# A new order inside the even attention steps of a two-layer encoder kernel

## The chip, the cores and the metric

The kernel runs on one core of a Trainium2 chip. The metric is device time in microseconds (us) of one execution of the whole program. Each kernel is run several times, and the median is given.

## What is computed

An encoder trunk of two layers over 1024 tokens of width 1024. Layer 0 mixes tokens by neighbourhood attention (mixer A), layer 1 by grouped-query attention (mixer B). Each layer is followed by an output projection and a gated per-layer embedding. The part that matters here is mixer B, for one block of 128 queries:

```python
def q_block(qb):          # 16 query heads in 4 groups, head dimension 64, 1024 keys
    sc = jnp.einsum('bkgqd,bksd->bkgqs', qb, k).astype(jnp.float32) * scale
    pr = jax.nn.softmax(sc, axis=-1).astype(v.dtype)
    return jnp.einsum('bkgqs,bksd->bkgqd', pr, v)
...
return (o * jax.nn.silu(gate)) @ w_out
```

q and k are RMS-normalised for each head and rotated by the token's row and column before this. All products are made at nearly full fp32 precision: each operand is split in a high and a low part (`h` and `l` in the tiles' names), and the products of the parts are summed.

## The kernel before

The program has four stages in a row: `mixer_a`, `dense_phase(0)`, `mixer_b`, `dense_phase(1)`. There is no automatic scheduler: every engine executes its instructions in the order in which the Python code issues them, and waits for the other engines by semaphores. So the order in which functions are called is the order of each engine's queue.

**Steps of mixer B.** The attention work is cut in 128 steps (`steps`, L1059). Step n is one head h, one half hf of the tokens and one tile t of 128 queries in this half; four steps in a row make one head's half, eight make a pair of heads' half. The functions of a step are

- `f_S` (L1061), the scores: four TensorE (PE) matmuls of 512 columns in a PSUM tile `s` (two buffers), and the row minimum `mn` on VectorE (DVE, L1071; q is negated, so that the minimum is the maximum);
- `f_E` (L1074), the exponential: ScalarE (ACT, L1077) reads `s` and `mn` and writes P, with the row's sum accumulated;
- `f_T` (L1080), P's transposes: eight PE transposes in two PSUM tiles `t` (L1087; the pool has two buffers), each tile copied by ACT to PTh (L1089) and the rest taken by DVE to PTl (L1090). PTh and PTl have room for two steps, an even and an odd one;
- `f_AV` (L1095), the product with v: sixteen PE matmuls for two steps at once, in the PSUM tile `o` (one buffer). It is issued in an even step n, for steps n-2 and n-1. Where it ends a head's half, `head_end` (L434) is called.
- `q_stack` (L1036), once in eight steps: four PE transposes of q (L1041) in a tile of the same pool `t`, an ACT copy (L1043), and, some issues later, the high part (ACT, L1050) and the low part (DVE, L1051) of the two tiles QS that the scores of the next eight steps read.

In step n the kernel issues T(n), E(n+1) and S(n+2). In even steps the order is AV, E, T, S; in odd steps T, E, S and, where (n + QS_AT) is a multiple of 8, `q_stack`.

**The end of a head.** `head_end` posts `evac`: ACT copies the lower half of `o` (L482), DVE adds the upper half (`join`, L446), which sets `o` free, and DVE takes the reciprocal of the row sums (L472). For the last pair of heads the reciprocal is spread (L459) and transposed by PE (`across`, L465) in another tile `o`.

**Dense work in between.** `mix` (L338) runs the list `att` of the steps' functions, each with a weight, and puts chunks of the dense work (projections of q, k, v, gate and of the embedding, in PSUM tile `d`, one buffer) between them: after each function it issues dense chunks until their share of the total is that of the weights so far. CB holds the weights of an even step's functions, CN those of an odd one. Each dense chunk is 6 or 12 matmuls; the last of a tile also issues the tile's copies on ACT.

**Pulses and the weight slot.** After each function `pulse` runs: `WQ.pump` may turn one staged weight tile (512 KB, loaded by a DMA in SP's queue) into its high part `wh` (ACT, L220), and issues the low part `wl` (DVE, L221) at the next pulse; `post.tick` counts down postponed work. `WQ.gate` says whether a weight may be split: None always, True yes, False only where a dense chunk needs it at once. In the loop it is True from an odd step's scores up to the next step's first function, so that a split falls right behind S(odd). From step 112 on it is None.

The lines that set the gate and the order, in short:

```python
te = [(f_T(n), w[2]), (f_E(n+1), w[3])]
if n % 2 == 0:
    te.reverse()
...
f_S(*steps[n + 2])
WQ.gate = n % 2 == 1 if n < 112 else None
```

Of the kernel before, what the change touches and what calls it, by code (L numbers as in the profile page):

```python
# [27 lines left out]
BIG = 1e30  # L28
WSLOTS = 4
CA = (1.0, 0.5, 1.25, 1.0, 0.75)  # L30
CB = (1.25, 1.0, 2.0, 0.5, 1.0)
CN = (1.5, 0.0, 1.0, 1.0, 1.5)
DG, DR, DQ, DY, NP = 1, 2, 2, 1, 8
KT, KN = 2, 4
DO = (2, 3)
DD = ((3, 2), (3, 2))
DT = (5, 2)
FIN = (4, 4)
# [1 line left out]
DP = 1  # L40
KD, KS = 3, 4
QD = (2, 5, 8)
QS_AT = 5
QO = (4, 6)
AGE, LAG = 3, 3
YS = (11, 11)
# [108 lines left out]
def trunk(ctx, tc, x, wts, rpb, gains, hgains, mask, rope, out):  # L155
# [21 lines left out]
    class Weights:  # L177
# [29 lines left out]
        def pump(self, force=False):  # L207
            self.clock += 1
            self.settle()
            self.stage(force)  # L210
            if self.split >= self.staged:
                return
            key, pid = self.q[self.split]
            if not force and self.gate is False:
                return
            if self.live[pid] >= self.cap[pid] or not (force or self.clock - self.st[key][1] >= self.age):
                return
            s, _ = self.st.pop(key)
            hi, lo = self.alloc[pid]()
            act.activation(hi, s, AF.Copy)  # L220
            self.rest = lambda: dve.tensor_tensor(lo, s, hi, ALU.subtract)  # L221
            self.tiles[key] = (hi, lo, pid)
            self.live[pid] += 1
            self.split += 1
            self.last = self.clock

        def settle(self):
            if self.rest:
# [17 lines left out]
    WQ = Weights()  # L246
# [187 lines left out]
    def head_end(sb, h, hf, rs, Ops, ylive, layer, gg, talloc):  # L434
        pair = h // 2
        b = (h % 2) * 64
        if h % 2 == 0:
            Y = sb.tile([128, 512], F32, name="Y", bufs=2)
            rb = sb.tile([128, 512], F32, name="rb", bufs=2)
            r8 = sb.tile([128, 8], F32, name="r8", bufs=4)  # L440
            ylive[pair, hf] = (Y, rb, r8, {})
        Y, rb, r8, tail = ylive[pair, hf]
        yh = Y[b:b + 64]

        def join():
            dve.scalar_tensor_tensor(yh, Ops[0:64], 0.5, yh, op0=ALU.mult, op1=ALU.add)  # L446

        def rows():
            r8T = sb.tile([128, 32], F32, name="r8T", bufs=2)
            dve.transpose(r8T.rearrange("p (a c) -> p a c", a=4), r8[:, None].to_broadcast([128, 4, 8]))  # L450
            rD = dram.tile([8, 128], F32, name="rD", bufs=4)
            for b in range(4):
                post.add(DD[layer][1], lambda b=b: sync.dma_start(rD[:, 32 * b:32 * b + 32], r8T[32 * b:32 * b + 8]))
            for i in range(2):
                post.add(DD[layer][1], lambda i=i: sync.dma_start(
                    rb[64 * i:64 * i + 64], bass.AP(tensor=rD.tensor, offset=rD.offset + 512 * i, ap=[[0, 64], [1, 512]])))

        def spread():
            dve.tensor_copy(rb.rearrange("p (t j c) -> p t j c", t=4, j=2),  # L459
                            r8.rearrange("p (j t) -> p t j", j=2)[:, :, :, None].to_broadcast([128, 4, 2, 64]))  # L460

        def across():
            ps = talloc()
            for t in range(4):
                pe.transpose(ps[:, t], rb[:, t * 128:(t + 1) * 128], ident)  # L465
            ps = ps.rearrange("p t c -> p (t c)")
            if hf == 0:
                act.activation(rb, ps, AF.Copy)
            tail["rb"] = rb if hf == 0 else ps

        def norm():
            dve.reciprocal(r8[:, 4 * (h % 2):4 * (h % 2) + 4], rs)  # L472
            if h % 2 == 0:
                return
            if pair < 7:
                post.add(DD[layer][0], rows)
            else:
                spread()
                post.add(DT[hf], across)

        def evac():
            act.activation(yh, Ops[64:128], AF.Copy, scale=0.5)  # L482
            post.add(DY, join)
            norm()
        if h == NH - 1 and hf == 1:
            evac()
        else:
            post.add(DO[layer], evac)
        if h % 2 == 0:
            return None  # L490
        G = gg.pop((pair, hf))
        del ylive[pair, hf]

        def fin_last():
            dve.tensor_tensor(Y, Y, G, ALU.mult)
            if "rb" not in tail:
                post.l = [e for e in post.l if e[1] is not across]
                across()
            dve.tensor_tensor(Y, Y, tail["rb"], ALU.mult)
            y3 = Y.rearrange("p (t c) -> p t c", t=4)  # L500
            ts = slice(4 * hf, 4 * hf + 4)
            act.activation(HTh[:, ts, 7, :], y3, AF.Copy)
            dve.tensor_tensor(HTl[:, ts, 7, :], y3, HTh[:, ts, 7, :], ALU.subtract)

        def fin():
            yhi, ylo = rb.bitcast(F32R), Y.bitcast(F32R)

            def store(c, src):
                sync.dma_start(yD[layer][c][4 * hf:4 * hf + 4, :, pair, :].rearrange("t p c -> p t c"),
                               src.rearrange("p (t c) -> p t c", t=4))  # L510

            def split():
                act.activation(yhi, Y, AF.Copy)
                dve.tensor_tensor(ylo, Y, yhi, ALU.subtract)
                post.add(2, lambda: (store(0, rb), store(1, Y)))
            pool.tensor_tensor(Y, Y, G, ALU.mult)
            pool.tensor_tensor(Y, Y, rb, ALU.mult)
            post.add(YS[layer], split)
        return fin_last if pair == 7 else fin
# [340 lines left out]
    def mixer_b(pend):  # L860
        with ExitStack() as es:
# [249 lines left out]
            pre = kv[:-2] + qi[:6] + kv[-2:-1] + qi[6:10] + kv[-1:] + qi[10:14]  # L1111
            fill = qi[14:] + [d for hf in range(2) for d in gate_items("bg", 0, hf, dalloc, sb, gg)]
            pre += [glue(lambda: q_stack(0, 0))] + fill[:5]
            pre += [glue(lambda: f_S(*steps[0]))] + fill[5:6] + [glue(lambda: f_E(*steps[0]))] + fill[6:7]
            pre += [glue(lambda: f_S(*steps[1]))] + fill[7:]
            for i, d in enumerate(pre):
                if i >= 2 and i % 2 == 0 and pend:
# [6 lines left out]
            for g in range(4):  # L1124
                att = []
                for n in range(32 * g, 32 * g + 32):
                    h, hf, t = steps[n]
                    av = n >= 2 and n % 2 == 0
                    w = CB if av else CN
                    def turn():  # L1130
                        if WQ.gate:
                            WQ.gate = False
                        later.tick()
                    att.append((turn, w[0]))
                    if av:
                        att.append((lambda n=n: f_AV(*steps[n - 1]), w[1]))
                    te = [(lambda n=n: f_T(*steps[n]), w[2])]
                    if n + 1 < len(steps):
                        te.append((lambda n=n: f_E(*steps[n + 1]), w[3]))
                    if n % 2 == 0:  # L1140
                        te.reverse()
                    att += te
                    if n + 2 < len(steps):
                        def scores(n=n):
                            f_S(*steps[n + 2])
                            WQ.gate = n % 2 == 1 if n < 112 else None
                        att.append((scores, w[4]))
                    m = n + QS_AT
                    if m % 8 == 0 and m < len(steps):
                        hn, fn, _ = steps[m]  # L1150
                        att.append((lambda hn=hn, fn=fn: q_stack(hn // 2, fn), 0.0))
                    if YLOAD_B <= n < YLOAD_B + NT:
                        att.append((lambda t=n - YLOAD_B: load_y(1, t), 0.0))
                if g == 3:
                    att.append((lambda: f_AV(*steps[-1]), CB[1]))
                def gates(p):
                    return [i for hf in range(2) for i in gate_items("bg", p, hf, dalloc, sb, gg)]
                dense = []
                if g > 0:
                    dense += left  # L1160
                if g < 3:
                    qi = q_items(g + 1, pool)
                    kv = kv_items(1, pool) if g == 1 else [None, None]
                    dense += kv[:-2] + qi[:KS] + [k for k in kv[-2:-1] if k] + qi[KS:8] + [k for k in kv[-1:] if k] + gates(2 * g + 1) + qi[8:]
                    left = gates(2 * g + 2)
                else:
                    WQ.cap[3] = 2
                    dense += gates(2 * g + 1) + pp_items(1, dalloc, sb, TAGS_B)
                mix(att, dense, hold=HOLD if g == 3 else 0)
# [170 lines left out]
```

## Time and profile before

| | before |
|---|---|
| median of 3 runs | 1563.97 us (1562.44 to 1564.62) |
| the profiled execution | 1560.76 us |
| its span, from the first to the last instruction | 1558.9 us |
| mean granted TensorE clock | 0.998 |
| loop of mixer B (first scores to the last product with v) | 784 to 1361 us of the span |
| TensorE busy from 1086 to 1221 us | 135.0 of 135.0 us |
| TensorE busy from 1221 to 1361 us | 134.83 of 140 us |

In the rows below, PE is TensorE, PEld its weight loads, DVE VectorE, ACT ScalarE, POOL GpSimd, SP SyncE. A row of the groups reads: line, engine, operation, what it writes and reads, shapes, count, then the busy time, the mean ns of one, and the engine's idle time before it with what ended it. A row of the waits reads: who waited for whom, us in total, times, longest. A row of the timeline begins with the start in us and the duration; in square brackets stand the engine's idle time before it and what ended it. Matmuls are pipelined, and their ends are modelled.

### The profile page before, as it was taken

What the parts mean: (1) busy time and instruction counts of PE and PEld (TensorE: products, weight loads), DVE (VectorE), ACT (ScalarE), POOL (GpSimd) and SP (SyncE); (2) the same over time, 40 slices, a digit from 0 to 9 for tenths busy, and PEclk for the clock granted to TensorE, in tenths of its full rate; (3) what the DMA queues carried; (4) which work ended last, traced back from release to release, by engine and by line L of the source; (5) the groups of instructions that cost most, each with busy time, mean ns of one, the idle gap of its engine ahead of it and who ended that gap; (6) DMA issues with size and microseconds to landing.
All of it is one profiled execution on the core that took longest, in us unless ns stands there. A gap on an engine that the chain in (4) does not pass through costs nothing.

```text
span 1558.9 us, 24287 instructions
## 1 busy us (share of the span) xinstructions
PE 1519.0 (97%) x9048; PEld 1327.7 (85%) x9048; DVE 1025.8 (66%) x2062; ACT 871.8 (56%) x1744; POOL 279.5 (18%) x372
## 2 busy tenths in 40 slices
PE   6999999999999999999999999999999999999997
PEld 5888988988988788888988889989999888788886
DVE  6576477377477436648877787777877877625636
ACT  6465466376366622434466776766767777622422
POOL 2111121112112010000222132443131200000023
PEclk9999999999999999999999999999999999999999
DMA  8212122132122972142210111111111113651213
GB/s 274 78 41 75 44 89 79 35 95 82 35 85 83 336 260 68 54 141 94 76 49 21 39 38 55 45 38 50 56 33 42 61 55 117 225 200 54 75 55 128
DMA packets 89861, 138.84 MB, mean 89 GB/s; under 512 B 16912, under 2 KB 55952, under 8 KB 89744
## 3 DMA queue, kind: packets, MB, share of 16 engines
q1 hardware_dynamic: 85136, 122.62, 24.3%
q10 hardware_dynamic: 4608, 14.68, 2.6%
q8 instruction: 71, 1.16, 0.3%
q14 instruction: 46, 0.38, 0.1%
HBM read 104.65 MB, written 36.15 MB: 90 GB/s over the span
## 4 chain that ended last, share of the span: by engine, by line
PE 43%; DVE 6%; ACT 3%; issue 2%; ACTq 0%; DVEq 0%
PE d L305 23%; PE o L305 7%; PE t L1087 6%; PE s L305 6%; DVE PTl L1090 1%; DVE mn L1071 1%; ACT PTh L1089 1%; ACT P L1077 1%; PE t L430 1%; PE t L1041 0%; DVE QS L1051 0%; DVE wl L221 0%; DVE t L905 0%; DVE KB L982 0%; DVE qt L906 0%
## 5 line engine op out<-in xcount | busy, mean ns | idle before, releaser
L305 PE MATMUL d<-wh,HTh 128*128 128x256 f32 (+1 forms) x1096 | 372.6, 340 | 4.8 <-ACT HTh L431 2.1
L305 PE MATMUL d<-wh,HTl 128*128 128x256 f32 (+1 forms) x1096 | 365.9, 334 | 1.5 <-DVE HTl L432 1.5
L305 PE MATMUL d<-wl,HTh 128*128 128x256 f32 (+1 forms) x1096 | 365.2, 333 | 0.0
L1090 DVE TENSOR_TENSOR PTl<-t,PTh 128x512 fp32r<-128x512 f32 x256 | 164.5, 684 | 107.1 <-ACT PTh L1089 106.7
L305 PEld LDWEIGHTS d<-wh,HTh 128*128 128x128 f32 x1096 | 207.9, 190 | 28.2 <-ACT HTh L431 2.7
L305 PEld LDWEIGHTS d<-wh,HTl 128*128 128x128 f32 x1096 | 207.8, 190 | 24.0 <-DVE HTl L432 2.2
L305 PEld LDWEIGHTS d<-wl,HTh 128*128 128x128 f32 x1096 | 208.2, 190 | 21.4
L305 PE MATMUL d<-HTh,wh 128*128 128x512 f32 x504 | 206.0, 409 | 0.0
L305 PE MATMUL d<-HTh,wl 128*128 128x512 f32 x504 | 197.8, 392 | 0.0
L305 PE MATMUL d<-HTl,wh 128*128 128x512 f32 x504 | 197.7, 392 | 0.0
L1077 ACT ACTIVATE P<-s,mn 128x1024 f32<-128x1024 f32 x128 | 142.8, 1116 | 56.6 <-DVE mn L1071 55.7
L1089 ACT ACTIVATE PTh<-t 128x512 fp32r<-128x512 f32 x256 | 140.1, 593 | 45.8 <-PE t L1087 45.3
L1071 DVE TENSOR_REDUCE mn<-s 128x1 f32<-128x1024 f32 x128 | 154.9, 1210 | 11.9 <-PE s L305 11.8
L1087 PE MATMUL t<-ident,P 128*128 128x128 f32 x1024 | 136.9, 274 | 6.6 <-DVE PTl L1090 4.8
L221 DVE TENSOR_TENSOR wl<-wstage,wh 128x1024 fp32r<-128x1024 f32 x89 | 115.1, 1298 | 42.3 <-ACT wh L220 42.1
L305 PE MATMUL s<-KA,QS 128*128 128x512 f32 (+2 forms) x384 | 133.5, 402 | 0.0
L1087 PEld LDWEIGHTS t<-ident,P 128*128 128x128 f32 x1024 | 114.8, 140 | 21.7 <-DVE PTl L1090 15.8
L305 PE MATMUL s<-KB,QS 128*128 128x512 f32 (+2 forms) x384 | 121.8, 371 | 0.0
L305 PE MATMUL o<-PTh,V 128*128 128x256 f32 (+2 forms) x672 | 118.8, 287 | 1.5 <-DVE Y L446 0.9
L305 PE MATMUL o<-PTl,V 128*128 128x256 f32 (+2 forms) x672 | 119.3, 289 | 0.4 <-DVE PTl L684 0.3
L684 DVE TENSOR_TENSOR PTl<-t,PTh 128x384 fp32r<-128x384 f32 (+1 forms) x128 | 66.6, 521 | 76.1 <-ACT PTh L683 75.0
L305 PEld LDWEIGHTS d<-HTh,wl 128*128 128x128 f32 x504 | 94.6, 188 | 21.8
(179 smaller groups left out, 2483.6 us busy)
## 6 DMA issues: line engine op xcount, KB each, us to landing
wstage<-in_wts SPq DMA_DIRECT2D x92, 512.0 KB
X<-in_x SPq DMA_DIRECT2D x16, 512.0 KB
pp<-ppD SPq DMA_DIRECT2D x32, 256.0 KB
rb<-rD SPq DMA_DIRECT2D x56, 128.0 KB
ppD<-th SPq DMA_DIRECT2D x20, 256.0 KB
xD<-X SPq DMA_DIRECT2D x8, 512.0 KB
X<-xD SPq DMA_DIRECT2D x8, 512.0 KB
yD0h<-rb SPq DMA_DIRECT2D x14, 256.0 KB
```

Source lines behind the costliest of these rows:

```text
L221: self.rest = lambda: dve.tensor_tensor(lo, s, hi, ALU.subtract)
L305: pe.matmul(ps, a, b, start=first, stop=last, skip_group_check=True)
L430: pe.transpose(ps[:, k], xn[:, (4 * c + k) * 128:(4 * c + k + 1) * 128], ident)
L684: dve.tensor_tensor(PTl[:, sl], ps[:, :m], PTh[:, sl], ALU.subtract)
L1071: dve.tensor_reduce(mn, ps, axis=AX.X, op=ALU.min)
L1077: act.activation(p, ps, AF.Exp, bias=mn, scale=-1.0, accum_out=RS[h, hf][:, t:t + 1])
L1087: pe.transpose(ps[:, i], p[:, k * 128:(k + 1) * 128], ident)
L1089: act.activation(PTh[:, ks, c], ps, AF.Copy)
L1090: dve.tensor_tensor(PTl[:, ks, c], ps, PTh[:, ks, c], ALU.subtract)
```

## The change

In even steps the exponential E(n+1) comes first, then (where due) q's transposes, then AV, T, S: `q_stack` moves from the end of an odd step to an even one (QS_AT 4 in place of 5). Odd steps keep T, E, S. The gate opens with an even step's E and closes with its T, and also closes after one split; it is closed too from the first scores in the prologue on. In layer 1 a head's end is evacuated two pulses after its last product instead of three (the same place, since E has left the row of functions in between), and the join is issued at once with it, ahead of the next scores' minimum, instead of one pulse later. The weights are put down anew as CE and CO; their sums for a pair of steps stay as they were, but the very last step's first function has the weight LAST, and the last product with v 1.5 instead of 1.0.

```diff
-CB = (1.25, 1.0, 2.0, 0.5, 1.0)
-CN = (1.5, 0.0, 1.0, 1.0, 1.5)
+CE = (1.25, 0.0, 1.5, 2.0, 1.0)
+CO = (1.5, 1.0, 1.0, 1.5)
+LAST = 4.0
-DO = (2, 3)
+DO = (2, 2)
-QS_AT = 5
+QS_AT = 4
...
             self.last = self.clock
+            if self.gate:
+                self.gate = False
...
             act.activation(yh, Ops[64:128], AF.Copy, scale=0.5)
-            post.add(DY, join)
+            if layer == 0:
+                post.add(DY, join)
             norm()
+            if layer == 1:
+                join()
...
-            pre += [glue(lambda: f_S(*steps[0]))] + fill[5:6] + [glue(lambda: f_E(*steps[0]))] + fill[6:7]
+            def first():
+                f_S(*steps[0])
+                WQ.gate = False
+            pre += [glue(first)] + fill[5:6] + [glue(lambda: f_E(*steps[0]))] + fill[6:7]
...
-                    h, hf, t = steps[n]
-                    av = n >= 2 and n % 2 == 0
-                    w = CB if av else CN
-                    def turn():
-                        if WQ.gate:
-                            WQ.gate = False
-                        later.tick()
-                    att.append((turn, w[0]))
-                    if av:
-                        att.append((lambda n=n: f_AV(*steps[n - 1]), w[1]))
-                    te = [(lambda n=n: f_T(*steps[n]), w[2])]
-                    if n + 1 < len(steps):
-                        te.append((lambda n=n: f_E(*steps[n + 1]), w[3]))
+                    def exp(n=n):
+                        f_E(*steps[n + 1])
+                        WQ.gate = n % 2 == 0 if n < 112 else None
+
+                    def turn(n=n):
+                        f_T(*steps[n])
+                        if WQ.gate:
+                            WQ.gate = False
+                    ahead = [exp] if n + 1 < len(steps) else []
+                    scores = [lambda n=n: f_S(*steps[n + 2])] if n + 2 < len(steps) else []
                     if n % 2 == 0:
-                        te.reverse()
-                    att += te
-                    if n + 2 < len(steps):
-                        def scores(n=n):
-                            f_S(*steps[n + 2])
-                            WQ.gate = n % 2 == 1 if n < 112 else None
-                        att.append((scores, w[4]))
-                    m = n + QS_AT
-                    if m % 8 == 0 and m < len(steps):
-                        hn, fn, _ = steps[m]
-                        att.append((lambda hn=hn, fn=fn: q_stack(hn // 2, fn), 0.0))
+                        fs = list(zip([later.tick] + ahead, CE))
+                        m = n + QS_AT
+                        if m % 8 == 0 and m < len(steps):
+                            hn, fn, _ = steps[m]
+                            fs.append((lambda hn=hn, fn=fn: q_stack(hn // 2, fn), 0.0))
+                        if n >= 2:
+                            fs.append((lambda n=n: f_AV(*steps[n - 1]), CE[2]))
+                        fs += zip([turn] + scores, CE[3:])
+                    else:
+                        fs = list(zip([later.tick, turn] + ahead + scores, CO))
+                        if n == len(steps) - 1:
+                            fs[0] = (later.tick, LAST)
+                    att += fs
...
-                    att.append((lambda: f_AV(*steps[-1]), CB[1]))
+                    att.append((lambda: f_AV(*steps[-1]), CE[2]))
```

## The prediction, made before the changed kernel ran

> **What bounds the kernel now.** The page's first part comes first, then the waits of TensorE inside mixer B's loop (from 760 us to 1370 us), since the change touches nothing else.
>
> ```profile
> PE 1519.0 (97%) x9048; PEld 1327.7 (85%) x9048; DVE 1025.8 (66%) x2062; ACT 871.8 (56%) x1744; POOL 279.5 (18%) x372
> ```
> ```profile
> PE t L1087 <- DVE PTl L1090: 4.8, 4, 1.6
> PE t L1041 <- DVE PTl L1090: 1.9, 4, 0.9
> PE t L1087 <- ACT th L976: 1.2, 2, 0.8
> PE o L465 <- DVE Y L446: 1.0, 1, 1.0
> PE o L305 <- DVE Y L446: 0.9, 2, 0.6
> ```
>
> TensorE (PE) is the bound: 1519.0 of 1558.9 us. In the loop its named waits are 4.8 + 1.9 + 1.2 + 1.0 + 0.9 = 9.8 us. The order of its work hardly changes, so the most that a better order can bring is about 10 us; what it can cost is open above. So the question is which PE waits go and which come.
>
> What sits just behind PE? The rows over the steps' stretch (795 to 1358 us) show the exponential E and its accumulator read:
>
> ```profile
> L1077 ACT ACTIVATE P<-s,mn 128x1024 f32<-128x1024 f32 x127 | 141.7, 1115 | 52.3 <-DVE mn L1071 51.4
> ...
> L1077 ACT ACTIVATION_READ_ACCUMULATOR P<-s,mn 128x1 f32 x127 | 25.1, 197 | 0.0
> ```
>
> ScalarE (ACT) stands idle 51.4 us ahead of E, and what ends the idleness is the row minimum `mn` on VectorE (DVE), not ACT's queue. Step 64 (write n for a step's number) shows the chain:
>
> ```profile
> 1086.22 1.07 ACT L220 ACTIVATE wh<-wstage 128x1024 fp32r<-128x1024 f32 x1
> 1087.98 1.12 ACT L1077 ACTIVATE P<-s,mn 128x1024 f32<-128x1024 f32 x1 [0.70 <-DVE mn L1071]
> 1088.99 0.19 ACT L1077 ACTIVATION_READ_ACCUMULATOR P<-s,mn 128x1 f32 x1
> 1089.09 1.08 ACT L1089 ACTIVATE PTh<-t 128x512 fp32r<-128x512 f32 x2
> ```
> ```profile
> 1086.73 1.22 DVE L1071 TENSOR_REDUCE mn<-s 128x1 f32<-128x1024 f32 x1
> ...
> 1088.01 1.22 DVE L221 TENSOR_TENSOR wl<-wstage,wh 128x1024 fp32r<-128x1024 f32 x1
> ...
> 1090.28 1.28 DVE L1090 TENSOR_TENSOR PTl<-t,PTh 128x512 fp32r<-128x512 f32 x2
> ```
> ```profile
> 1088.33 1.04 PE L1087 MATMUL t<-ident,P 128*128 128x128 f32 x8
> ...
> 1091.52 1.03 PE L1087 MATMUL t<-ident,P 128*128 128x128 f32 x8
> ```
>
> The minimum for step 65 ends at 1087.95. E(65) starts at once, though it was queued behind the products with v. The weight's high part `wh` ran in the 1.8 us before it in which ACT had nothing else (1.07 and the 0.70 of waiting), and the low part `wl` on DVE beside E. Then follow PTh(64), PTl(64) and, in the same PSUM buffer, the transposes T(65) at 1091.52. The weight work is hidden completely.
>
> **The change part by part.** The profiled execution took 1560.76 us (span 1558.9, 1.9 around it), 3.2 under the median 1563.97; the terms are differences of stalls, so I add the sum to the median.
>
> *The exponential first.* E(n+1) moves ahead of AV in even steps. As it waits for `mn`, which nothing moves forward, it starts when it started: 0 us. The cover for this zero is DVE. But ACT runs in order, so all that was issued between S(n+1) and E now stands behind a wait for `mn`: q's copy and the weight's `wh`.
>
> *q's transposes* now stand behind the odd step's dense chunk instead of right behind the scores. Of their 1.9 us of waiting, the share stays where the weights of the order put no chunk in front (steps 4 and 100, by counting chunks against CE and CO); I count 1.5 us gained at n = 12, 20, 28, bounds 0 and 1.9. QS itself is read two steps later, so making it later costs nothing while a step lasts 3.2 us (T(64) to T(65), 1088.33 to 1091.52).
>
> But the copy L1043 that empties q's PSUM tile is now queued behind E. The pool `t` has two buffers: T(n-1) took both, q one, T(n) takes the other and then q's. So T(n)'s second half waits for mn, E, accumulator read, copy. Steps 84 and 52:
>
> ```profile
> 1171.31 0.60 ACT L1043 ACTIVATE th<-t 128x512 f32<-128x512 f32 x1 [0.42 <-PE t L1041]
> 1172.33 1.11 ACT L1077 ACTIVATE P<-s,mn 128x1024 f32<-128x1024 f32 x1 [0.42 <-DVE mn L1071]
> 1173.34 0.19 ACT L1077 ACTIVATION_READ_ACCUMULATOR P<-s,mn 128x1 f32 x1
> ```
> ```profile
> 1173.03 1.04 PE L1087 MATMUL t<-ident,P 128*128 128x128 f32 x8
> ```
> ```profile
> 1026.63 1.12 ACT L1077 ACTIVATE P<-s,mn 128x1024 f32<-128x1024 f32 x1 [0.67 <-DVE mn L1071]
> ```
> ```profile
> 1027.02 1.03 PE L1087 MATMUL t<-ident,P 128*128 128x128 f32 x8
> ```
>
> Step 84: E with its read ends at 1173.34 + 0.19 = 1173.53, 1.2 us after it began, and the copy would end at 1174.13; the second half of T begins at 1173.03 + 1.04/2 = 1173.55: 0.6 us of new wait. Step 52: 1026.63 + 1.2 + 0.6 = 1028.43 against 1027.54: 0.9 us. Of the 15 such steps about half come out near nothing by the same sum, the rest between 0.1 and 0.9: I take 3 us, bounds 0 and 15 x 0.9 = 13. The Trainium skill, "PSUM — Partial Sum Buffer", section "Summary: rules for kernel authors", says to evacuate PSUM promptly; a copy that waits for an exponential does the opposite. By that rule the term stands nearer 13 than 3; the rows of the slack say 3.
>
> *The weight slot.* Now `wh` may follow E(n+1) and `wl` goes to DVE one issue later, both ahead of PTh(n) and PTl(n). In 795 to 1290 us the splits are
>
> ```profile
> L220 ACT ACTIVATE wh<-wstage x15: 1042/1064/1072, 794.4 to 1257.6; 128x1024 fp32r<-128x1024 f32 x15
> L220 ACT ACTIVATE KA<-wstage x2: 1067/1068/1068, 1229.6 to 1238.5; 128x1024 fp32r<-128x1024 f32 x2
> ```
>
> so 17. From `mn`'s end to the release of T(n+1)'s buffer a split step now needs E with its read 1.2, wh 1.06, wl 1.22, half of PTl 0.64: 4.1 us. It has, at step 64, 1091.52 - 1087.95 = 3.6: a loss of 0.5. Steps 96 and 38:
>
> ```profile
> 1222.24 1.22 DVE L1071 TENSOR_REDUCE mn<-s 128x1 f32<-128x1024 f32 x1
> ```
> ```profile
> 1226.80 1.03 PE L1087 MATMUL t<-ident,P 128*128 128x128 f32 x8
> ```
> ```profile
> 955.18 1.21 DVE L1071 TENSOR_REDUCE mn<-s 128x1 f32<-128x1024 f32 x1
> ```
> ```profile
> 961.14 1.04 PE L1087 MATMUL t<-ident,P 128*128 128x128 f32 x8
> ```
>
> Step 96 has 3.3 us: it loses 0.8. Step 38, with a dense chunk on each side of its scores, has 4.8 and loses nothing. Four of the 17 lie like step 38; the 13 others lose 0.5 to 0.8, a mean of 0.65: 8.5 us. After a stall DVE and ACT have caught up on PE, and five splits follow each other every second step from n = 96: I take 7, bounds 0 and 17 x 0.8 = 14. The DMA that refills the staging buffer moves with the split, in SP's queue; no wait for it stands among the rows, so 0. That no split may come after the first scores in the prologue moves one of the 17, no more.
>
> *Heads joined at once.* The join (L446) goes ahead of the minimum instead of behind it, and the one buffer `o` comes free 1.2 us sooner. The two waits on L446 above, 1.0 + 0.9, go: 1.9 us gained, bounds 0 and 1.9. The minimum put behind it serves a step two later, so nothing is late next.
>
> *The end of the loop.* LAST and the new sums of weights put a chunk between the scores and T(125), and between T(126) and T(127):
>
> ```profile
> 1344.88 0.63 ACT L502 ACTIVATE HTh<-Y 128x512 fp32r<-128x512 f32 x1 [2.32 <-DVE Y L499]
> ...
> 1345.90 1.11 ACT L1077 ACTIVATE P<-s,mn 128x1024 f32<-128x1024 f32 x1
> ...
> 1348.36 0.93 PE L1087 MATMUL t<-ident,P 128*128 128x128 f32 x5 [1.56 <-DVE PTl L1090]
> ```
> ```profile
> 1357.17 1.26 PE L1087 MATMUL t<-ident,P 128*128 128x128 f32 x8 [1.04 <-DVE PTl L1090]
> ```
>
> ```profile
> 1353.85 1.42 PE d L305 x6
> ```
>
> T(127)'s 1.04 is covered by a chunk of 1.42 us; as that chunk's copy then stands before PTh(127), I count 0.9. T(125)'s 1.56 hangs on E(125), which still stands behind L502, whose end is 1344.88 + 0.63 = 1345.51: E(125) moves from 1345.90 by 0.4 at most, and I count 0.3. I take 1.2, bounds 0 and 2.6.
>
> *Sum:* -1.5 - 1.9 - 1.2 + 3 + 7 = +5.4, so **1569.4 us**. All gains and no loss: 1.9 + 1.9 + 2.6 = -6.4, 1557.6.
>
> **The rivals.** *A, the new waits stay off PE (faster).* In the chain from mn to T(n+1), DVE loses `wl` ahead of other small work, and the minimum comes 0.6 us or more earlier in split steps. From that point 4.1 us fit into the gap of step 64, the splits and copies cost 0 to 1, and the gains of 4.6 stand: 1560, and to 1557 with all gains. For it speak the 9.8 us of waits, several of which the change addresses by name; against it, that mn(65) follows PTl(63), which follows T(63) on PE, so that nothing on DVE is spare. By the Trainium skill, "Perfetto Trace Analysis", section "Optimization Strategy", one finds the gaps of the saturated engine and lets what they wait for start sooner; this is what the join and the chunks at the end do, and by it A would be the case. Chance 0.27.
>
> *B, gains and losses cancel (within 0.2%).* The splits fall to the steps with slack, or `wl` lands behind PTl because a split is ready only one issue later: the splits then cost 2 instead of 7, and the sum is 0.4: 1564.4. Chance 0.18.
>
> *C, more is queued behind E.* The chunk's own PSUM tile `d` has one buffer, and its copy, issued behind E and `wh`, frees it 1 us later where a tile ends between AV and T; 1 us at six steps on top of the sum is +11.4: 1575.4. Against it: in the second and fourth quarter of the heads T mostly follows AV directly. Chance 0.13.
>
> That the change does not do what it says is inside the forecast: the exponential is first in the queue, not in time.
>
> **How the numbers follow.** Forecast 0.42 (own range 1567 to 1573), A 0.27, B 0.18, C 0.13. A measurement here tells about 0.2% (3 us) from no change. Slower: 0.42 + 0.13 = 0.55; the same 0.18; faster 0.27. The range from 1557 to 1577 leaves out the upper part of C and little of A.
>
> **What would show it.** Right: in an even step with a split, ACT reads E, wh, PTh without a pause, and T(n+1) waits for PTl; T in steps 52 and 84 shows its eight transposes in two groups with a wait on L1043; the waits of PE on L446 are gone; the wait of E on `mn` is as large or larger. Wrong: E(n+1) starts well ahead of T(n)'s transposes, or the sum of PE's waits on L1090 in the loop is under 5 us.

## The result and the profile after

| | before | after |
|---|---|---|
| median, same chip, 6 runs each | 1562.38 us (1561.96 to 1564.62) | 1569.73 us (1569.41 to 1573.3) |
| the profiled execution | 1560.76 us | 1569.74 us |
| its span | 1558.9 us | 1567.9 us |
| mean granted TensorE clock | 0.998 | 0.998 |

The change makes the kernel slower: 1.0049 times the time before, with a 95% interval of 1.0036 to 1.0062. That is 7.35 us between the medians, where the prediction had 5.4. The forecast of 1569.4 us lies so near to the measured time partly because it was put on the first median of before, 1563.97 us, which three more runs moved to 1562.38.

The first part of the page of after: TensorE (PE) is still the bound.

```profile
PE 1522.1 (97%) x9048; PEld 1329.1 (85%) x9048; DVE 1029.6 (66%) x2062; ACT 874.1 (56%) x1744; POOL 275.2 (18%) x372
```

The waits of PE in mixer B's loop of after (760 to 1380 us; each row: who waited for whom, us in total, times, longest). Line numbers moved: T is now L1093, PTl L1096, q's transposes L1047, q's copy L1049, k's copy L982.

```profile
PE t L1093 <- DVE PTl L1096: 8.9, 12, 1.6
PE t L1093 <- ACT th L1049: 3.1, 7, 1.1
PE t L1093 <- ACT th L982: 2.5, 2, 2.3
PE d L308 <- ACT th L560: 0.7, 1, 0.7
...
PE t L1047 <- DVE PTl L1096: 0.2, 1, 0.2
```

The wait for PTl has grown from 4.8 to 8.9 us. The wait for q's copy is new (3.1), that for k's copy went from 1.2 to 2.5. q's transposes wait 0.2 instead of 1.9, and the waits on the join (1.0 + 0.9 in before) are gone. So the forecast gains came, and the new waits are larger than they.

How much of the time is this? The group of P's transposes T in the same window holds both what PE waited ahead of them and their own duration; first before, then after:

```profile
L1087 PE MATMUL t<-ident,P 128*128 128x128 f32 x1024 | 136.9, 274 | 6.6 <-DVE PTl L1090 4.8 <-ACT th L976 1.2
```
```profile
L1093 PE MATMUL t<-ident,P 128*128 128x128 f32 x1024 | 140.4, 276 | 15.1 <-DVE PTl L1096 8.9 <-ACT th L1049 3.1 <-ACT th L982 2.5
```

8.5 us more of waiting and 3.5 us more of busy time: 12.0 us lost at T, against a net loss of 7.35. Much of the 3.5 us is waiting too, inside a row of T, and a part is a lower clock at one place (both below).

The exponential's row from 795 to 1366 us of after shows that it did not start sooner: its wait for the minimum is larger, 70.9 us against 52.3.

```profile
L1083 ACT ACTIVATE P<-s,mn 128x1024 f32<-128x1024 f32 x127 | 141.7, 1115 | 70.9 <-DVE mn L1077 70.3
```

What ACT did before in that idle time, `wh` above all, now runs behind the wait. Step 66 of after, ACT, then DVE, then PE:

```profile
1101.54 1.12 ACT L1083 ACTIVATE P<-s,mn 128x1024 f32<-128x1024 f32 x1 [1.42 <-DVE mn L1077]
1102.56 0.19 ACT L1083 ACTIVATION_READ_ACCUMULATOR P<-s,mn 128x1 f32 x1
1102.65 1.05 ACT L221 ACTIVATE wh<-wstage 128x1024 fp32r<-128x1024 f32 x1
1103.60 1.07 ACT L1095 ACTIVATE PTh<-t 128x512 fp32r<-128x512 f32 x2
```
```profile
1100.27 1.18 DVE L1077 TENSOR_REDUCE mn<-s 128x1 f32<-128x1024 f32 x1
1103.73 1.23 DVE L222 TENSOR_TENSOR wl<-wstage,wh 128x1024 fp32r<-128x1024 f32 x1 [2.28 <-ACT wh L221]
1104.87 1.28 DVE L1096 TENSOR_TENSOR PTl<-t,PTh 128x512 fp32r<-128x512 f32 x2
```
```profile
1105.61 1.26 PE L1093 MATMUL t<-ident,P 128*128 128x128 f32 x8 [1.05 <-DVE PTl L1096]
```

ACT idles 1.42 us, then runs E(67), wh, PTh(66) without a pause; wl idles DVE for 2.28 us until wh is there; PTl(66) follows, and T(67) waits 1.05 us for it. From the end of the minimum (1100.27 + 1.18 = 1101.45) to T(67) at 1105.61 it is 4.16 us: the chain that the prediction put at 4.1.

### The profile page after: what moved, and what is told of

Its sections match the earlier page's. It is cut to its first block, busy times and chain, and to the rows that moved or that the text cites. A ratio compares the mean times of both kernels' runs of the same rounds, so it can differ in the third digit from the quotient of the medians.

```text
span 1567.9 us, 24280 instructions
## 1 busy us (share of the span) xinstructions
PE 1522.1 (97%) x9048; PEld 1329.1 (85%) x9048; DVE 1029.6 (66%) x2062; ACT 874.1 (56%) x1744; POOL 275.2 (18%) x372
## 4 chain that ended last, share of the span: by engine, by line
PE 39%; DVE 7%; ACT 5%; issue 2%; DVEq 0%; ACTq 0%
PE d L308 21%; PE o L308 6%; PE t L1093 6%; PE s L308 5%; DVE PTl L1096 2%; DVE mn L1077 2%; ACT P L1083 1%; ACT wh L221 1%; DVE wl L222 1%; PE t L433 1%; ACT PTh L1095 0%; ACT th L532 0%; ACT G L531 0%; DVE ss L924 0%; DVE KB L988 0%
## 5 line engine op out<-in xcount | busy, mean ns | idle before, releaser
L1096 DVE TENSOR_TENSOR PTl<-t,PTh 128x512 fp32r<-128x512 f32 x256 | 165.3, 684 | 92.5 <-ACT PTh L1095 91.5
L1093 PE MATMUL t<-ident,P 128*128 128x128 f32 x1024 | 140.4, 276 | 15.1 <-DVE PTl L1096 8.9
L1093 PEld LDWEIGHTS t<-ident,P 128*128 128x128 f32 x1024 | 114.5, 141 | 34.1 <-DVE PTl L1096 22.2
```

The lines of the kernel that those rows point to most:

```text
L1093: pe.transpose(ps[:, i], p[:, k * 128:(k + 1) * 128], ident)
L1096: dve.tensor_tensor(PTl[:, ks, c], ps, PTh[:, ks, c], ALU.subtract)
```

## The experiments

The theory: the loss is what now stands in ACT's queue behind an exponential that waits for its minimum, the weight slot first (`wh`, and `wl` behind it on DVE), q's copy second. The rivals: that the new place of the exponential costs by itself; and that only the low part `wl` ahead of PTl matters, as the prediction's rival B had it. The runs of before beside these kernels had medians of 1561.6 to 1561.9 us; ratios are to these, with 95% intervals.

**The weight slot put back.** The changed kernel, with the gate opened at an odd step's scores and closed by the next step's first function, as before; its two other closings (after one split, and in the prologue) are taken out too, and all else stays.

```diff
                         f_E(*steps[n + 1])
-                        WQ.gate = n % 2 == 0 if n < 112 else None
...
+                    def score(n=n):
+                        f_S(*steps[n + 2])
+                        WQ.gate = n % 2 == 1 if n < 112 else None
```

> The changed kernel with the weight slot put back where it was: the gate opens at an odd step's scores and closes at the next step's first function; the two other closings (after one split, in the prologue) are taken out too. Theory S (a weight's high part queued between the exponential and P's copies costs most): the waits of TensorE at the split steps go, some 8 to 9 us of the changed kernel's 1569.7, so 1560 to 1562, and the wait on the minimum ahead of the exponential gets shorter. Rival P (the exponential's early place costs, because the copies of the dense tiles are queued behind it): 1568 to 1570. Rival J (the join ahead of the minimum costs): 1569 to 1570.

1557.46 us (1556.39 to 1558.71), 0.997 (0.9958 to 0.9982): the slot costs 1569.73 - 1557.46 = 12.3 us of the changed kernel, which without it beats before. T's group in this kernel's loop is shorter than in after by 8.7 us of waits and 2.7 of busy time:

```profile
L1091 PE MATMUL t<-ident,P 128*128 128x128 f32 x1024 | 137.7, 274 | 6.4 <-DVE PTl L1094 3.3 <-ACT th L1047 1.5 <-ACT th L980 1.1
```

Step 66 on ACT shows where the weight work went: `wh` runs ahead of E, in time that is idle anyway.

```profile
1094.24 1.05 ACT L221 ACTIVATE wh<-wstage 128x1024 fp32r<-128x1024 f32 x1
1095.76 1.12 ACT L1081 ACTIVATE P<-s,mn 128x1024 f32<-128x1024 f32 x1 [0.47 <-DVE mn L1075]
```

**q's transposes ahead of the exponential.** The changed kernel; in an even step q_stack is called before E, so its copy doesn't queue behind E.

```diff
-                            fs.append((lambda hn=hn, fn=fn: q_stack(hn // 2, fn), 0.0))
+                            fs.insert(1, (lambda hn=hn, fn=fn: q_stack(hn // 2, fn), 0.0))
```

> The changed kernel with q's transposes and their copy issued ahead of the exponential in even steps, not behind it; TensorE's own order stays. Theory S: the waits of P's transposes on q's copy (3.1 us named on TensorE in the trace of the changed kernel) go: 1566 to 1567. Rival P: as q's copy is one of several, 1568 to 1570. If the place of q in TensorE's row were the cost, and not the copy, nothing changes: 1569.7.

1573.36 us (1571.67 to 1575.12), 1.0071 (1.0059 to 1.0083): a miss, slower still. The wait on q's copy is gone, but with the earlier call everything that q_stack posts comes one pulse earlier too. The low part of QS slips ahead of a minimum on DVE; first this kernel, then after, at step 6 (timeline rows):

```profile
821.18 0.69 DVE L1057 TENSOR_TENSOR QS<-th,QS 64x512 fp32r<-64x512 f32 x1
821.79 1.21 DVE L1077 TENSOR_REDUCE mn<-s 128x1 f32<-128x1024 f32 x1
```
```profile
819.57 1.23 DVE L1077 TENSOR_REDUCE mn<-s 128x1 f32<-128x1024 f32 x1
820.83 0.69 DVE L1057 TENSOR_TENSOR QS<-th,QS 64x512 fp32r<-64x512 f32 x1
```

That was a guess from the rows, so it got a run of its own: the same kernel, the QS parts back at their old pulses.

```diff
-QO = (4, 6)
+QO = (5, 7)
```

> As e2 (q's transposes and copy ahead of the exponential), but with the two postponements of QS one pulse longer, so that its high and low parts stand where the changed kernel has them. Theory S: e2 was slower only because QS's low part slid ahead of the row minimum; with it back, the 3.1 us of waits on q's copy are gained: 1566.5 to 1568.5. Rival: the place of the copy ahead of the exponential is itself the cost: 1572 or more, like e2.

1568.02 us (1566.59 to 1569.58), 1.0037 (1.0025 to 1.005): the slip of QS cost 1573.36 - 1568.02 = 5.3 us, and q's copy behind E costs 1569.73 - 1568.02 = 1.7 us. The intervals of these two runs overlap, but their profiles bear the size out: the starts of T move apart by 0.97, 0.37, 0.41 and 0.37 us just behind the copies of steps 52, 68, 84 and 108, and by 1.8 us over the loop.

**Both undone.** The slot put back and q ahead of the exponential: the first two diffs above together, at first without the third (QO), then with it.

> The changed kernel with both of these: the weight slot put back and q ahead of the exponential. What stays of the change is the exponential ahead of the product with v, the join at once and the new weights of the order. Theory S: the two costs add up, only the gains are left: 1558 to 1560, faster than the kernel before by 2 to 4 us. Rivals P and J: still slower than the kernel before, 1565 or more.

1559.73 us (1558.44 to 1561.39), 0.9983 (0.9974 to 0.9991).

> e1 (slot put back) with q ahead of the exponential and QS's parts kept at their place. Theory S: e1's 1557.5 less the 1.5 us of waits on q's copy that its trace names: 1555.5 to 1557. Rival: as with e3, 1559 to 1560.

1555.26 us (1554.61 to 1556.89), 0.9958 (0.9945 to 0.997). This version beats both kernels, before by 6.4 us (1561.64 beside it) and after by 14.5. T's group in its loop:

```profile
L1091 PE MATMUL t<-ident,P 128*128 128x128 f32 x1024 | 136.2, 274 | 4.7 <-DVE PTl L1094 3.2 <-ACT th L980 1.1
```

**The exponential first, alone.** The kernel before, with E ahead of AV in even steps and the head's end at two pulses; first so, then with the store of a finished pair of heads (YS) at its old place. The weights of the order are put down anew, with the sum ahead of T as it was:

```diff
-CB = (1.25, 1.0, 2.0, 0.5, 1.0)
+CB = (1.25, 1.5, 2.0, 0.0, 1.0)
...
-DO = (2, 3)
+DO = (2, 2)
...
                     if n % 2 == 0:
                         te.reverse()
+                    if av:
+                        te.insert(1, (lambda n=n: f_AV(*steps[n - 1]), w[1]))
```

> The kernel before with one part of the change alone: in even steps the exponential is issued ahead of the product with v; slot, q's place, join and the place of the head's end stay as they were. Theory S: as the exponential waits for the minimum, nothing gained and nothing lost: within 1 us of the kernel before (1562). Rival P: slower by 4 us or more.

1569.28 us (1568.0 to 1572.72), 1.0047 (1.0035 to 1.0059): a miss by 7 us, and at first it looks as if the exponential itself were dear. ACT at step 14, before and then this kernel:

```profile
850.71 0.62 ACT L513 ACTIVATE rb<-Y 128x512 fp32r<-128x512 f32 x1
853.80 1.12 ACT L1077 ACTIVATE P<-s,mn 128x1024 f32<-128x1024 f32 x1 [2.47 <-DVE mn L1071]
```
```profile
854.55 1.11 ACT L1077 ACTIVATE P<-s,mn 128x1024 f32<-128x1024 f32 x1 [2.99 <-DVE mn L1071]
...
855.65 0.62 ACT L513 ACTIVATE rb<-Y 128x512 fp32r<-128x512 f32 x1
856.17 1.07 ACT L1089 ACTIVATE PTh<-t 128x512 fp32r<-128x512 f32 x2
```

The split of a finished pair (L513, and L514 on DVE) is posted by a count of pulses, and with E ahead of AV its pulse falls behind E: again a piece of work that had run in the idle time now stands between E and PTh. The second kernel counts one pulse less:

```diff
-YS = (11, 11)
+YS = (11, 10)
```

> As e4 (the kernel before with the exponential first in even steps), but the split of a finished pair of heads, which is posted by a count of pulses, comes one pulse earlier, so that it stands ahead of the exponential again as in the kernel before. Theory S: the exponential's place costs nothing by itself; what cost 7 us in e4 was that this copy (0.6 us on ScalarE) and its low part slid behind it: 1561 to 1564. Rival P (the copies of the dense tiles behind the exponential): 1567 to 1569, as e4.

1562.57 us (1561.52 to 1565.37), 1.0005 (0.9996 to 1.0014). Exponential first is worth nothing by itself, and what falls behind it is worth 6.7 us.

**Only wl behind PTl.** The changed kernel, with the gate opened at the products instead of at E: `wh` still stands ahead of PTh, `wl` behind PTl.

```diff
-                        WQ.gate = n % 2 == 0 if n < 112 else None
+                        WQ.gate = False if n < 112 else None
+
+                    def products(n=n):
+                        f_AV(*steps[n - 1])
+                        WQ.gate = True if n < 112 else None
...
-                            fs.append((lambda n=n: f_AV(*steps[n - 1]), CE[2]))
+                            fs.append((products, CE[2]))
```

> The changed kernel with the gate opened one function later, at the product with v instead of the exponential: the weight's high part stays between the exponential and PTh on ScalarE, but its low part is issued behind PTl on VectorE. Theory S: the chain from the minimum to the buffer's release loses 1.22 of its 4.1 us and fits the 3.3 to 3.6 us of the gap; most of the slot's 12 us go: 1560 to 1563. Rival W (ScalarE's 1.06 us is the cost by itself): 1566 to 1569.

1571.0 us (1570.08 to 1571.54), 1.0056 (1.0043 to 1.0068): a miss, no gain at all. DVE at step 66, between two minima:

```profile
1099.53 1.18 DVE L1077 TENSOR_REDUCE mn<-s 128x1 f32<-128x1024 f32 x1
1103.48 1.29 DVE L1096 TENSOR_TENSOR PTl<-t,PTh 128x512 fp32r<-128x512 f32 x2 [2.77 <-ACT PTh L1095]
1104.68 1.22 DVE L222 TENSOR_TENSOR wl<-wstage,wh 128x1024 fp32r<-128x1024 f32 x1
1105.82 1.22 DVE L1077 TENSOR_REDUCE mn<-s 128x1 f32<-128x1024 f32 x1
```

PTl now follows PTh at once, yet from the minimum's end (1100.71) to PTl it still is 2.77 us, of which wh is 1.05; in after it was 1104.87 - 1101.45 = 3.42. Only 0.65 us is gained, since the half of PTh that PTl has to wait for ran beside wl before. And `wl` now stands ahead of the next minimum with its 1.22 us: q's transposes wait 3.4 us for PTl in this kernel's loop, where they waited 0.2 in after. So the rival falls that only the place of `wl` ahead of PTl matters. How the cost divides between `wh` and `wl` is not shown, as no run has one of them behind the wait without the other.

**Single parts on the kernel before.** First the slot behind E, with E still behind AV:

```diff
+            if self.gate:
+                self.gate = False
...
+                        WQ.gate = n % 2 == 0 if n < 112 else None
```

> The kernel before with the weight slot alone moved behind the exponential of even steps (closed by P's transposes, after one split and from the prologue's first scores on); the exponential stays behind the product with v. Theory S, as corrected by e10 (ScalarE's 1.06 us between the exponential and PTh is the price, and the delays go on from one split to the next): 7 to 11 us slower, 1569 to 1573. Rival (the slot costs only together with the exponential's early place): within 3 us of the kernel before.

1574.99 us (1574.33 to 1575.76), 1.0083 (1.0069 to 1.0096): 13.1 us, more than expected. Here too `wl` falls behind PTl, and what it delays shows among PE's waits of this kernel: the join, on which PE waited 1.0 + 0.9 us in before.

```profile
PE o L307 <- DVE Y L448: 4.9, 5, 2.3
```

The join at once:

```diff
-            post.add(DY, join)
+            if layer == 0:
+                post.add(DY, join)
             norm()
+            if layer == 1:
+                join()
```

> The kernel before with one part alone: in layer 1 a head's join is issued at once, ahead of the next scores' minimum. Theory S: TensorE's two waits on the join (0.9 and 1.0 us) go: 1.9 us faster, 1559.5 to 1560.5. Rival J: the minimum is pushed back by 0.7 us, and the exponential with it: the kernel before or up to 3 us slower.

1561.6 us (1560.94 to 1563.54), 0.9997 (0.9988 to 1.0006): a miss, nothing gained. Where PE had waited 1.0 us ahead of `across` (L465), it now waits 1.4 us just after it, for the copy of that tile, which stands behind an exponential on ACT; ACT and then PE of this kernel:

```profile
1331.37 1.11 ACT L1080 ACTIVATE P<-s,mn 128x1024 f32<-128x1024 f32 x1 [0.38 <-DVE mn L1074]
...
1332.48 0.59 ACT L468 ACTIVATE rb<-o 128x512 f32<-128x512 f32 x1
```
```profile
1333.12 1.21 PE L305 MATMUL o<-PTh,V 128*128 128x256 f32 x8 [1.45 <-ACT rb L468]
```

In before the products at this place began at 1332.91. The join was not the last thing to arrive.

The weights at the loop's end:

```diff
-                    att.append((turn, w[0]))
+                    att.append((turn, w[0] if n < 127 else 4.0))
...
-                    att.append((lambda: f_AV(*steps[-1]), CB[1]))
+                    att.append((lambda: f_AV(*steps[-1]), 1.5))
```

> The kernel before with the new weights at the end of the order alone (4.0 for the last step's first function, 1.5 for the last product with v). Theory S: 1.2 us faster, at most 2.6 us: 1559.2 to 1560.8. Rival: the chunk that is put in front of the last transposes only moves the wait: within 0.5 us of the kernel before.

1561.14 us (1560.2 to 1565.19), 0.9996 (0.9987 to 1.0005): 0.7 us, inside the interval. The two waits at the end are gone, but the chunks that cover them are taken from elsewhere, and a new wait stands there, in this kernel's timeline of PE:

```profile
1318.20 1.26 PE L1087 MATMUL t<-ident,P 128*128 128x128 f32 x8 [1.74 <-DVE PTl L1090]
```

Last, the best kernel with the join one pulse later again, to see whether the join is worth something in the new order:

```diff
-            if layer == 0:
-                post.add(DY, join)
+            post.add(DY, join)
             norm()
-            if layer == 1:
-                join()
```

> The changed kernel with the weight slot put back behind the odd step's scores and q's transposes ahead of the exponential (their QS parts at their old places), which took 1555.26 us, with one part undone: the join is issued one pulse after the evacuation again, behind the next minimum, as in the kernel before. Theory 1 (the join's term of the prediction stands, 1.9 us, but only in an order in which nothing else waits for what the join releases): 1557.2 us, and TensorE waits on the join again, 1 to 2 us in all. Theory 2 (the join gives nothing in any order, as when it was done alone, 1561.6 against 1561.9 us): 1555.3 us, within 1 us, and the waits on the join come back while waits on the rowsums' spread tile go.

1555.83 us (1554.53 to 1557.56), 0.9962 (0.9948 to 0.9975): 0.6 us slower than with it, not to be told from nothing. One of the waits on the join is back, 1.2 us ahead of `across`, though it shows in the time with 0.6 us at most. Two products had waited 0.9 us for the join in before; here they don't, though the join is late. On DVE, before and then this kernel, at step 21:

```profile
882.17 0.68 DVE L1051 TENSOR_TENSOR QS<-th,QS 64x512 fp32r<-64x512 f32 x1
882.88 0.68 DVE L446 SCALAR_TENSOR_TENSOR Y<-o,Y 64x512 f32<-64x512 f32 x1
```
```profile
880.81 0.67 DVE L447 SCALAR_TENSOR_TENSOR Y<-o,Y 64x512 f32<-64x512 f32 x1
...
882.71 0.68 DVE L1052 TENSOR_TENSOR QS<-th,QS 64x512 fp32r<-64x512 f32 x1
```

In before, the low part of QS stood ahead of the join; q's new place puts it behind. So at this place the gain that the prediction gave to the join belongs to q's move.

## Why the prediction was right, and where its sizes were off

The forecast held in its sign and its mechanism. That the sum came so near is partly luck: the slot's term was 5.3 us too low, q's copy 1.3 too high and the gains 1.8 too low, so three errors mostly made up for each other.

*The exponential first, 0 us: right,* by the run that moves E alone and keeps the posted work (1.0005). The reason given holds: E's idle time ahead of it, ended by the minimum, grew. But the zero hangs on a condition that the prediction did not name: that no posted work changes its place past E. Where the store's split does, it costs 6.7 us. In the changed kernel q_stack's call in the even step gives one more pulse, and the store keeps its place.

*The weight slot, 7 us: right in mechanism, mis-sized.* It is 12.3 us taken out of the changed kernel and 13.1 put into the kernel before. The starts of T, step by step, show where: in the profile of after they fall behind those of the run with the slot put back by 13.3 us in all (the profile of that run is its fastest execution, hence 13.3 and not 12.3). The splits of steps 34, 38 and 48 cost nothing, that of step 50 costs 3.2 us, and the thirteen others cost 10.0 together, 0.77 each: 1.1 and 1.5 at steps 64 and 66, 4.8 at the five from step 96 on, 0.3 at step 32, about 0.5 at each of the rest. So fourteen splits cost something where the prediction counted thirteen, and three things are missing from the 7.

First, the discount "after a stall DVE and ACT have caught up on PE" is wrong. DVE in after, behind step 64's split:

```profile
1093.75 1.22 DVE L222 TENSOR_TENSOR wl<-wstage,wh 128x1024 fp32r<-128x1024 f32 x1 [1.30 <-ACT wh L221]
...
1095.18 1.28 DVE L1096 TENSOR_TENSOR PTl<-t,PTh 128x512 fp32r<-128x512 f32 x2
...
1096.88 0.68 DVE L449 SCALAR_TENSOR_TENSOR Y<-o,Y 64x512 f32<-64x512 f32 x1
1097.59 1.23 DVE L1077 TENSOR_REDUCE mn<-s 128x1 f32<-128x1024 f32 x1
```

Until the minimum of step 66's split, 1100.27, no row has an idle bracket: DVE works without a pause. PE stands still for the stall, but DVE does not get ahead in it, because it is the one that is late. So step 66 begins with its minimum ending at 1101.45, 0.23 us behind the start of T(66) at 1101.22, where in before it ended at 1095.21 + 1.18 = 1096.39, 0.20 ahead of T(66) at 1096.59. The five splits from n = 96 show the same over a longer stretch. This is T in after from 1230 to 1276 us, with its waits (us, times); the run with the slot put back has none in the same steps.

```profile
its engine sat idle before it (us, times) until:
  DVE PTl L1096: 3.8, 4
  ACT th L1049: 0.6, 1
```

That is 4.4 us of named waits for five splits, 0.88 each, where the prediction had 0.65 ahead of its discount. The 0.6 on q's copy counts among them because that copy stands behind `wh` there.

Second, PE loses more than the wait named ahead of a row. At step 64 the forecast was 0.5 and the wait is 0.67, but the eight transposes behind it, T(65), also take 1.25 us instead of 1.03. The weight loads of T(65) show why: the second four wait once more, for the second half of PTl.

```profile
1095.92 1.25 PE L1093 MATMUL t<-ident,P 128*128 128x128 f32 x8 [0.67 <-DVE PTl L1096]
```
```profile
1095.92 0.42 PEld L1093 LDWEIGHTS t<-ident,P 128*128 128x128 f32 x4 [1.10 <-DVE PTl L1096]
1096.52 0.42 PEld L1093 LDWEIGHTS t<-ident,P 128*128 128x128 f32 x4 [0.18 <-DVE PTl L1096]
```

From the start of T(64) to the scores behind T(65) it is 1096.93 - 1091.90 = 5.03 us, in before 1092.31 - 1088.33 = 3.98: 1.05 us lost, where the prediction counted the release of the first half alone, and 0.5. The splits of steps 58, 72 and 88 have no named wait of PE at all, only such waits of the weight loads, and still cost 0.5 each.

Third, k's copy: at n = 50 it stands behind E and wh, and the second half of T waits for it, 2.28 us where before had 0.31 and the run with the slot put back 0.81. It is the same mechanism on a PSUM copy that the prediction did not count. What follows the wait was not foreseen at all: the granted clock reads 0.50 for the next 3 us. First the wait, then the row of that stretch (from and to, length, PE busy, instructions, granted clock, DMA share, GB/s):

```profile
1018.04 1.11 PE L1093 MATMUL t<-ident,P 128*128 128x128 f32 x4 [2.28 <-ACT th L982]
```
```profile
1018.00:1021.10 3.10, 3.06 (x15) 0.50 0.72 227
```

The products on `d` start 0.21 us apart there, 0.12 us in the run with the slot put back. From this half of T(50) to T(51) PE needs 1023.75 - 1018.04 = 5.71 us, in that run 4.26. So of the 3.2 us that step 50 costs, about half is the longer wait (2.28 - 0.81) and about half the lower clock (5.71 - 4.26).

*q's copy behind E, 3 us: right in mechanism, too high.* It is 1.7 us. Step 52 shows it, ACT and then PE; T comes in two groups of four:

```profile
1028.93 1.12 ACT L1083 ACTIVATE P<-s,mn 128x1024 f32<-128x1024 f32 x1 [2.08 <-DVE mn L1077]
...
1030.04 0.59 ACT L1049 ACTIVATE th<-t 128x512 f32<-128x512 f32 x1
```
```profile
1029.32 0.60 PE L1093 MATMUL t<-ident,P 128*128 128x128 f32 x4
1030.68 0.65 PE L1093 MATMUL t<-ident,P 128*128 128x128 f32 x4 [0.76 <-ACT th L1049]
```

0.76 us against 0.9 foreseen; step 84 has 0.19 against 0.6. The Trainium skill, "PSUM — Partial Sum Buffer", section "Summary: rules for kernel authors", asks for prompt evacuation; the runs bear its sign out, but the size is nearer the sum of the slack in each step than the upper bound of 13.

*The gains, 4.6 us: too low in sum, and not right in parts.* The best kernel, which has the gains and neither of the two losses, is 6.4 us faster than before. The waits of the join (1.9) and at the end of the loop (2.6) are gone from after, as foreseen; but made alone on the kernel before, the join moves the time by 0 and the end by 0.7 us, because in each case another wait ends just as late. In the new order those other waits aren't there. By the terms as measured, 12.3 + 1.7 - 6.4 = +7.6, against 7.35; this shows that the two losses add up, not what the gains consist of.

*The rivals.* A had the minimum come 0.6 us sooner in split steps, with `wl` no longer ahead of it. It doesn't: at step 64 it ends 0.37 us ahead of T(64) in after (1090.31 + 1.22 against 1091.90) and 0.38 in before (1087.95 against 1088.33), and at step 66 it is later than in before, as said above. B had `wl` land behind PTl, and the splits cost 2 us. The run that does this takes 1571.0 us, so the place of `wl` does not decide. C (tile `d` freed late) shows one wait of 0.7 us on L560 in after; before and the best kernel have the same 0.7 us on that copy, so it is no cost of the change.

What stays open is how the best kernel's 6.4 us divide between q's place, the end of the loop and the rest: the single parts give less on the kernel before than together. The two profiles say only where the time is gained: from T(0) to T(120) the best kernel is 3.7 us faster than before, and from T(120) to T(127) another 3.1; it began the loop 1.4 us later in its profile. The refill DMA of the staging buffer, put at 0, was not tried by itself.

## What to carry to other kernels

An instruction that waits closes its queue: moving it ahead gained nothing here (1.0005), as what it waits for came no sooner, and it turned what was issued behind it from work in idle time to work on the chain (12.3 us for the weight slot). So list what ran in the idle time ahead of the waiting instruction, and price each piece as if it stood on the path, with the carry-over from one to the next if the late engine has no pause between them. Then compare the starts of the same instruction in two traces, as the sum of the named waits leaves a part of the loss out (8.7 of 13.3 us at T here). Where work is placed by counts of calls, a moved call moves other work too; correct the counts before judging the move, as two runs here were off by 5 to 7 us for that alone.

## What the runs showed of the hardware

A stop of PE cost more than the wait that the trace names ahead of a row. At step 64 it is 1.05 us by the starts, for a named wait of 0.67. Of the rest, 0.22 us stands inside T's row, whose second four transposes wait for the second half of PTl (0.18 us by their weight loads). The other 0.16 us comes from where the idle time is counted: from the modelled end of the product before, 1094.86 + 0.40 = 1095.26, while in the stream the next instruction started 0.23 us behind that product's start, at 1095.09.

One longer stop also cost clock. The granted clock fell to 0.50 for about 3 us after the wait of 2.28 us on k's copy in after, and again after the same wait in the two runs that have q ahead of the exponential and the slot behind it. In the loops of the other kernels no stretch of 2 us reads under 0.9, although one of them has a wait of 2.26 us for a join. So these runs don't show what decides it.
